# Strassen products for the gates: pairs in one bank, sums of h on VectorE, and transfers for sums sent singly

## The chip, the cores and the metric

The kernel runs on one core of a Trainium2 chip. A core has TensorE (PE in the profile; its weight loads, which overlap the matmuls, are listed as PEld), VectorE (DVE), ScalarE (ACT), GpSimd (POOL) and SyncE (SP), which here only sends transfers. Each engine works through its own list of instructions in order; semaphores hold an instruction back until what it needs is there, and everything behind it on that engine then waits too. Transfers are sent from the queues of SP, ScalarE and GpSimd; those that add to what stands in memory (accumulating transfers) are sent from GpSimd. The metric is device time in microseconds (us); lower is better.

## The reference

One layer of an encoder, for 1024 rows of 1024 float32 numbers:

```python
h = rmsnorm(x, g_mix)
z = h @ w_in                    # columns: 512 pooling, 1024 q, 1024 k, 1024 v
y_pool = pool_mixer(z[:, :512], w_pool_grp, pool_scale)
y_attn = diff_attention(q, k, v, ...)   # 8 heads, two softmax maps each
gates  = sigmoid(h @ w_gate + b_gate)   # 1024x1024 by 1024x2048
merged = gates[:, :1024] * (y_pool @ w_branch_pool) + gates[:, 1024:] * (y_attn @ w_branch_attn)
x = x + merged @ w_out
x = x + square(relu(rmsnorm(x, g_ffn) @ w_up)) @ w_down
```

q and k are normalised by head: each of the 64-element pieces is divided by the root of its mean square plus 1e-6. The change concerns `h @ w_gate` and this head norm.

## The kernel before

**Matmuls.** Each float32 operand is split in two parts of reduced precision, hi (a cast, on ScalarE) and lo (the source less hi, on VectorE unless an engine is given: `split`). A product is three matmuls (`mm3`, lines 140 to 142): hi·hi, hi·lo, lo·hi. All operands have h transposed (`hT[kp, th, hl]`: four pairs of 128-row blocks, two halves of 512 tokens, hi and lo).

**Stages.** The first part, some 710 us, is the attention: a loop over steps `g` = −2 to 73, one step for each of 64 pairs of a head and a tile of 128 tokens. In a step several stages of different tiles are issued, each a fixed number of steps behind the first: `A` computes z (q, k, v of a tile), `B` (`stage_prep`) normalises q and k and splits V, `C` (`stage_qkT`) transposes them, `D` makes scores, `E` transposes the softmax, `F` multiplies with V, `R` normalises. After it come the two branches, the merge with the gates, the output projection and the MLP, which the change leaves alone.

**Fillers.** Between these stages of the attention the loop takes units from a generator, `fillers`, at `F_PACE` units a step from step `F_FROM` on and up to `F_UNITS`; what is left runs behind the loop (the tail). The units are four pooling groups (U, two pairs of units) and the gate products. A scheduler that simulates a timeline then sets each engine's order from all that has been issued.

**The gate products.** `h @ w_gate` is done by Strassen's scheme with 7 products in place of 8 blocks: product 1 to 7 for each of eight column tiles `c`, 12 matmuls of 128x512 each (4 blocks × 3). Products 1, 2 and 3 take blocks of h itself; 5, 6, 7 and 4 take sums of h. The weights of 1, 2 and 4 are blocks of `w_gate`; those of 5, 6, 7 and 3 are sums `gw_sum` 1 to 4, made in memory by a copy (`c`, sent by SP) and an accumulating transfer (`a`, sent by GpSimd; 2 MB each). `h` in `G_SUMS` stores a quarter of h: hi by SP, then lo added by GpSimd. `t_set` (lines 439 and following) loads two such quarters (`rT`), subtracts one from the other on GpSimd and splits the result into the operand `T`, lo on GpSimd too; t6, t4 and t7 build on `t2_dram`, which t5 writes and one accumulating transfer completes.

**What a product does.** `gate_product` loads the weights (`frg`, line 462, on SP), splits them (`fwg`: cast on ScalarE, lo on GpSimd), runs 12 matmuls into one PSUM bank of the fillers, copies the bank to `go` (line 476, ScalarE) and sends it to the quadrants `q` of `gd[c]` that need it: product 1 writes all four (from ScalarE's queue), the others add to what is there (line 483, from GpSimd). `G_TO` says which quadrants. From unit 42 on, a second and third bank are used (`spare_bank`).

**The head norm.** In `stage_prep`, ScalarE squares q and k of a tile (`sq`), VectorE sums each 64 (`ms`), `rsq` multiplies by 1/64 and adds 1e-6 on VectorE (line 282), GpSimd raises to the power −0.5 (line 283), and VectorE multiplies (`qn`, line 801).

```python
O = "B1 C2 H7 D4 R8 E5 F6 W-2 A0"
F_FROM, F_PACE, F_UNITS, F_SPARE = 4, 1.0, 60, 58
```

`O` gives the stages in the order in which a step issues them, with the number of steps by which each lags.

Of the kernel before, what the change touches and what calls it, by code (L numbers as in the profile page):

```python
# [17 lines left out]
P = 128  # L18
# [47 lines left out]
def encoder_kernel(  # L66
# [321 lines left out]
    def gate_sums(what):  # L388

        def wq(i, j):  # L390
            return w_gate[j * 512 : (j + 1) * 512, i * D : (i + 1) * D]

        def copy(i, src):
            with tc.issue_after(marks["SP"]):
                nc.sync.dma_start(gw_sum[i], src)

        def acc(i, src):
            with tc.issue_after(marks["POOL"]):
                nc.gpsimd.dma_start(gw_sum[i], src, accum_op=ALU.add)

        n = int(what[1])
        if what[0] == "h":
            kh, th = divmod(n, 2)
            for hl in range(2):
                for kp in (2 * kh, 2 * kh + 1):
                    dst = h_dram[kh][th][kp % 2 * 256 : kp % 2 * 256 + 256, :].rearrange("(i p) c -> p i c", p=P)
                    with tc.issue_after(marks["POOL" if hl else "SP"]):
                        if hl:
                            nc.gpsimd.dma_start(dst, f(hT[kp, th, 1]), accum_op=ALU.add)
                        else:  # L410
                            nc.sync.dma_start(dst, f(hT[kp, th, 0]))
        elif what[0] == "c":
            copy(what[1], (None, wq(1, 0), gw_sum["1"], wq(1, 0), gw_sum["2"])[n])
        else:
            acc(what[1], (None, wq(1, 1), wq(0, 0), wq(0, 0), wq(0, 1))[n])
# [3 lines left out]
    def t_set(j):  # L419

        for k in range(4):
# [6 lines left out]
            hi, lo = t[:, 0, :], t[:, 1, :]  # L428
            rw = raw([P, S], f"rT{j}_{k}")
            a, b = rw[:, 0:512], rw[:, 512:S]  # L430
            if j == "6":
                nc.sync.dma_start(a, t2_dram[rows, :])
            else:
                sa, sb = {
                    "5": (h_dram[0][0], h_dram[0][1]), "7": (h_dram[1][1], h_dram[0][1]), "4": (t2_dram, h_dram[1][0]),
                }[j]
                nc.sync.dma_start(a, sa[rows, :])
                nc.sync.dma_start(b, sb[rows, :])
                nc.gpsimd.tensor_tensor(a, a, b, op=ALU.subtract)
# [6 lines left out]
    g_unit = [0]  # L446

    def gate_product(j, c):
# [9 lines left out]
        with ExitStack() as later:  # L458
            if n < 3:
                later.enter_context(tc.issue_after(h_hi[n + 2].ins))  # L460
                later.enter_context(tc.issue_after(loads["x3"].ins))
# [3 lines left out]
        ps = (spare_bank if n >= F_SPARE - 16 else fill_bank)(f"g{j}_{c}")  # L465
        for k in range(4):
            if j in "123":
                b = [hT[k // 2 + 2 * (j != "1"), int(j == "3"), hl][:, k % 2, :] for hl in range(2)]
            else:
                b = pair(T[j, k])  # L470
            mm3(ps, w[:, 0, k, :], w[:, 1, k, :], *b, k == 0, k == 3)
        fo = fo_tile(f"go{j}_{c}")
        if j == "6":
            nc.scalar.activation(fo[:, 0:512], ps, AF.Copy, scale=-1.0)
        else:
            nc.scalar.copy(fo[:, 0:512], ps)  # L476
        q0, q1 = G_TO[j]
        dst = gd[c][q0:q1].rearrange("q p t -> p q t")
        from_ = fo[:, 0:512].unsqueeze(1).broadcast_to([P, q1 - q0, 512])
        if j == "1":  # L480
            nc.scalar.dma_start(dst, from_)
        else:
            nc.gpsimd.dma_start(dst, from_, accum_op=ALU.add)  # L483

    def fillers():
        turn, step, groups = {}, 0, 0
        for w in G_PLAN.split():
            if w[0] == "t":
                fw_all[0] = False
                t_set(w[1])  # L490
                continue
            if step in G_SUMS:
                gate_sums(G_SUMS[step])
            step += 1
            if w == "U":
# [3 lines left out]
            else:  # L499
                gate_product(w, turn.setdefault(w, 0))  # L500
                turn[w] += 1
                yield 1
# [4 lines left out]
    with ExitStack() as ph:  # L507
# [282 lines left out]
        def stage_prep(h, t):  # L790
# [19 lines left out]
        def stage_qkT(h, t):  # L810

            th, c0 = t // 4, (t % 4) * P
            if t == 0:
                gghs[h] = sp.tile([P, 1], F32, tag="ggh", name=f"ggh{h}", bufs=2)
# [201 lines left out]
        for g in range(-2, N + 10):  # L1016
# [10 lines left out]
            if g == G_COLS:  # L1027
                columns()
            gens = {}
# [8 lines left out]
            while made < F_UNITS and made < (g - F_FROM) * F_PACE:  # L1038
                made += next(units)
        for _ in units:  # L1040
# [675 lines left out]
```

## Time and profile before

| | |
|---|---|
| time, median of 3 runs | 1572.9 us (1569.59 to 1573.69) |
| the profiled execution | 1573.15 us, span 1571.4 us |
| mean granted TensorE clock | 0.989 |
| busy: TensorE, VectorE, ScalarE, GpSimd | 1520.1, 1075.2, 831.0, 487.7 us |
| transfers | 275.63 MB |

How to read the rows shown below: a row of groups is "line engine operation, out<-in, shape, count | busy us, mean ns | idle time of the engine just ahead of them, and what ended it". A row of waits is "who <- for whom: us in all, count, longest". A row of the chain is "start, length, what", and of the timeline "start, length, what [idle before <- what ended it]". Names are those of the program, with the numbers of buffers left out. A row of transfers ends with KB each and the median us from issue to landing.

### The profile page before, as it was taken

How to read it: one execution, taken by the hardware profiler on the slowest of the kernel's cores; microseconds unless marked ns; L12 is line 12 of the kernel's file. 1: busy time of each engine (PE TensorE's matmuls, PEld its weight loads, DVE VectorE, ACT ScalarE, POOL GpSimd, SP SyncE). 2: the span in 40 equal slices, each digit the busy share in tenths (PEclk: the TensorE clock that was granted, in tenths of full speed). 3: DMA queues.
4: the chain of work that ended last, by engine and by line, in shares of the span. 5: the costliest groups of instructions: out<-in, count | busy, mean ns of one | idle time of the engine just before them, and what ended most of it. 6: DMA issues, size and time to landing. Idle time of an engine off the chain costs nothing.

```text
span 1571.4 us, 21898 instructions
## 1 busy us (share of the span) xinstructions
PE 1520.1 (97%) x7542; PEld 1309.3 (83%) x7542; DVE 1075.2 (68%) x2137; ACT 831.0 (53%) x1717; POOL 487.7 (31%) x515
## 2 busy tenths in 40 slices
PE   9999999999899998988899999999999999999999
PEld 8888988889799987977788887888888878888887
DVE  7687778676677776773474789867675577646662
ACT  6556565564566665664353458556555544333331
POOL 3434334362656455465874630000000000000000
PEclk9999999999999999999999999999999999999999
DMA  7633554386676666479963743555533689637750
GB/s 243 228 75 96 141 184 128 95 194 123 167 157 129 115 128 160 89 180 261 381 220 111 249 161 113 174 169 162 169 137 123 239 300 360 233 129 244 224 199 27
DMA packets 206297, 275.63 MB, mean 175 GB/s; under 512 B 11973, under 2 KB 119210, under 8 KB 206122
## 3 DMA queue, kind: packets, MB, share of 16 engines
q1 hardware_dynamic: 172810, 212.32, 40.8%
q0 software_dynamic: 16336, 34.61, 14.2%
q10 hardware_dynamic: 17040, 27.31, 4.7%
q8 instruction: 59, 0.97, 0.2%
q14 instruction: 52, 0.43, 0.1%
HBM read 186.08 MB, written 105.94 MB: 186 GB/s over the span
## 4 chain that ended last, share of the span: by engine, by line
PE 73%; DMA 9%; DVE 8%; POOL 3%; ACT 3%; issue 3%; SPq 1%; POOLq 0%; ACTq 0%; DVEq 0%
PE z L140 4%; PE z L141 4%; PE z L142 4%; PE Da L141 4%; PE Da L142 4%; PE Da L140 4%; PE Db L142 3%; PE Db L141 3%; PE Db L140 3%; PE X L140 3%; PE X L142 2%; PE X L141 2%; PE g L140 2%; PE g L141 2%; PE g L142 2%
## 5 line engine op out<-in xcount | busy, mean ns | idle before, releaser
L140 PE MATMUL z<-wqkv,hT 128*128 128x384 f32 x512 | 176.6, 345 | 7.1 <-DVE qn L801 6.1
L141 PE MATMUL z<-wqkv,hT 128*128 128x384 f32 x512 | 175.6, 343 | 0.0
L142 PE MATMUL z<-wqkv,hT 128*128 128x384 f32 x512 | 175.3, 343 | 0.0
L876 ACT ACTIVATE s<-s,nm 128x256 f32<-128x256 f32 (+7 forms) x128 | 99.9, 781 | 66.4 <-DVE nm L868 65.7
L283 POOL TENSOR_TENSOR ms<-ms,mhalf 128x4 f32<-128x4 f32 x64 | 68.1, 1064 | 143.5 <-DVE ms L282 140.7
L140 PEld LDWEIGHTS z<-wqkv,hT 128*128 128x128 f32 x512 | 97.8, 191 | 11.8 <-issue 5.7
L141 PEld LDWEIGHTS z<-wqkv,hT 128*128 128x128 f32 x512 | 97.7, 191 | 3.9 <-POOL wqkv L134 0.4
L142 PEld LDWEIGHTS z<-wqkv,hT 128*128 128x128 f32 x512 | 97.5, 191 | 2.8 <-DVE hT L531 0.5
L134 POOL TENSOR_TENSOR fwg<-frg,fwg 128x512 fp32r<-128x512 f32 x56 | 90.1, 1610 | 25.5 <-ACT fwg L133 25.5
L868 DVE CUSTOM_DVE_ANT_0 s<-sc,dist 128x512 f32<-128x512 f32 (+3 forms) x128 | 74.1, 584 | 22.3 <-PE sc L866 17.3
L865 PE MATMUL sc<-K,Q 128*128 128x512 f32 (+2 forms) x192 | 69.4, 363 | 8.5 <-DVE Q L836 6.3
L483 POOL DMA_DIRECT2D gd<-go x48 | 54.6, 1138 | 44.3 <-ACT go L476 26.2
L134 DVE TENSOR_TENSOR AS<-s,AS 128x512 fp32r<-128x512 f32 x64 | 43.4, 687 | 32.7 <-ACT AS L133 32.7
L866 PE MATMUL sc<-K,Q 128*128 128x512 f32 (+2 forms) x192 | 65.3, 347 | 0.0
L134 POOL TENSOR_TENSOR wqkv<-rqkv,wqkv 128x384 fp32r<-128x384 f32 x56 | 61.4, 1194 | 11.5 <-ACT wqkv L133 10.5
L140 PE MATMUL g<-T,fwg 128*128 128x512 f32 x128 | 51.6, 404 | 3.6 <-ACT fwg L133 3.6
L141 PE MATMUL ba<-yT,wba 128*128 128x512 f32 x128 | 50.7, 397 | 4.1 <-DVE yT L134 4.1
L142 PE MATMUL g<-T,fwg 128*128 128x512 f32 x128 | 51.7, 404 | 0.7 <-POOL fwg L134 0.7
L801 DVE TENSOR_TENSOR qn<-z,ms 128x256 f32<-128x256 f32 x64 | 26.9, 420 | 37.2 <-POOL ms L283 22.2
L141 PE MATMUL g<-T,fwg 128*128 128x512 f32 x128 | 51.2, 400 | 0.0
L142 PE MATMUL ba<-yT,wba 128*128 128x512 f32 x128 | 50.5, 395 | 0.0
L921 PE MATMUL ta<-identf,s 128*128 128x128 f32 x288 | 45.4, 276 | 4.9 <-DVE s L885 3.2
(498 smaller groups left out, 4913.3 us busy)
## 6 DMA issues: line engine op xcount, KB each, us to landing
wd<-in_w_down_dram SPq DMA_DIRECT2D x56, 512.0 KB, 5.4
wu<-in_w_up_dram SPq DMA_DIRECT2D x32, 512.0 KB, 4.5
udS<-us SPq DMA_DIRECT2D x64, 256.0 KB, 3.1
ur<-udS SPq DMA_DIRECT2D x32, 512.0 KB, 4.4
rqkv<-in_w_in_dram SPq DMA_DIRECT2D x64, 192.0 KB, 4.6
ur<-ud SPq DMA_DIRECT2D x24, 512.0 KB, 3.5
gd<-go ACTq DMA_DIRECT2D x8, 1024.0 KB, 8.4
gw_sum<-in_w_gate_dram POOLq DMA_DIRECT2D x4, 2048.0 KB, 16.1
```

The source lines that it names most:

```text
L134: (lo_eng or nc.vector).tensor_tensor(lo, src, f(hi), op=ALU.subtract)
L140: nc.tensor.matmul(ps, lhs_hi, rhs_hi, start=first, stop=False, **kw)
L141: nc.tensor.matmul(ps, lhs_hi, rhs_lo, start=False, stop=False, **kw)
L142: return nc.tensor.matmul(ps, lhs_lo, rhs_hi, start=False, stop=last, **kw)
L283: marks["POOL"] = nc.gpsimd.tensor_tensor(dst, dst, mhalf[:, :n], op=ALU.pow).ins
L483: nc.gpsimd.dma_start(dst, from_, accum_op=ALU.add)
L801: nc.vector.tensor_tensor(qn, z[:, 0:256].rearrange("p (a b) -> p a b", a=4), ms.unsqueeze(2).broadcast_to([P, 4, HD]), op=ALU.mult,)
L865: nc.tensor.matmul(dst, Q[:, i, 0, :], rhs, start=True, stop=False)
L866: nc.tensor.matmul(dst, Q[:, i, 1, :], rhs, start=False, stop=True)
L868: nc.vector.tensor_tensor_reduce(out=s[i][:, c : c + w], in0=sc[:, 0:w], in1=dist[:, o0 + c : o0 + c + w], scale=2.0 ** -(h + 1), scalar=B ...
L876: nc.scalar.activation(s[i][:, 0:n], s[i][:, 0:n], AF.Exp, bias=last, scale=-1.0, accum_out=Z[:, i, t : t + 1])
L921: nc.tensor.transpose(ta[:, i * P : (i + 1) * P], a[:, (4 * j + i) * P : (4 * j + i + 1) * P], identf)
```

## The change

1. Two pairs of products share a bank. Products 1 and 2 of a column tile (unit `A`), and products 5 and 3 (unit `B`), run one behind the other: the bank is copied out after the first, and the second then accumulates on top, so that its copy holds their sum. Products 1 and 2 become plain writes from ScalarE's queue (quadrants 1 to 3, and 0); products 5 and 3 add to one quadrant each.
2. `t_set` subtracts and splits on VectorE.
3. The transfers for sums are tied to steps of the main loop (9 to 29), not to units: eight stores of hi (`h`) and eight of lo (`i`) instead of four with two of each, and each weight sum accumulated in two halves of 1 MB.
4. Product 3 comes with product 5, and a unit that does nothing (`.`) stands ahead of each set of sums. Pace 1.03 and 62 units; the spare banks are used in the tail alone.
5. In `stage_prep`, `sq` has a 65th column that holds 1e-6 and stays; the square is scaled by 64 to the power −0.5; the sum over 65 columns is then ready for the power, and the multiply on VectorE is dropped.
6. `ggh` is allocated ahead, with 32 elements of padding: the tiles allocated after it start at a multiple of 64 bytes, where they started 32 bytes off one.

```diff
-F_FROM, F_PACE, F_UNITS, F_SPARE = 4, 1.0, 60, 58
-G_PLAN = "1 1 1 1 U 1 U 1 U 1 U 1 2 2 2 2 2 2 2 2 3 3 t5 3 5 5 5 5 5 5 5 5 t6 3 3 6 6 6 6 6 6 6 6 t4 3 3 4 4 4 4 4 4 4 4 t7 3 7 7 7 7 7 7 7 7"
-G_SUMS = {3: "h0", 5: "c1", 6: "h1", 8: "a1", 10: "h2", 11: "c2", 12: "c3", 13: "h3", 15: "a2", 17: "a3", 18: "c4", 20: "a4"}
-G_TO = {"1": (0, 4), "6": (1, 4), "7": (2, 4), "5": (1, 3), "2": (0, 1), "3": (1, 2), "4": (3, 4)}
+F_FROM, F_PACE, F_UNITS = 4, 1.03, 62
+G_PLAN = "A A A U A U A U A U A A . tB B B B B B B B B . t6 6 6 6 6 6 6 6 6 . t4 4 4 4 4 4 4 4 4 . t7 7 7 7 7 7 7 7 7"
+G_SUMS = {
+    9: "h0", 10: "i0 c1", 11: "h1", 12: "i1 a10", 13: "a11", 14: "h2", 15: "i2 c2", 16: "h3", 17: "i3 c3", 18: "a20",
+    19: "a21", 20: "h4", 21: "i4 a30", 22: "a31", 23: "h5", 24: "i5 c4", 25: "h6", 26: "i6 a40", 27: "a41", 28: "h7", 29: "i7",
+}
+G_TO = {"1": (1, 4), "2": (0, 1), "6": (1, 4), "7": (2, 4), "5": (2, 3), "3": (1, 2), "4": (3, 4)}
...
+            r = slice(int(what[2]) * 256, int(what[2]) * 256 + 256)
             with tc.issue_after(marks["POOL"]):
...
+                nc.gpsimd.dma_start(gw_sum[what[1]][r, :], src[r, :], accum_op=ALU.add, max_dma_last_dim=1024)
...
-                nc.gpsimd.tensor_tensor(a, a, b, op=ALU.subtract)
+                nc.vector.tensor_tensor(a, a, b, op=ALU.subtract)
             if j == "5":
                 nc.sync.dma_start(t2_dram[rows, :], a)
-            split(hi, lo, a, nc.gpsimd)
+            split(t[:, 0, :], t[:, 1, :], a)
...
+    def gate_unit(js, c):
+
+        ws = [gate_weights(j, c) for j in js]
+        ps = (spare_bank if in_tail[0] else fill_bank)(f"g{js}_{c}")
+        for n, (j, w) in enumerate(zip(js, ws)):
+            for k in range(4):
...
+                mm3(ps, w[:, 0, k, :], w[:, 1, k, :], *b, k == 0 and n == 0, k == 3, n > 0)
+            fo = fo_tile(f"go{j}_{c}")
...
+            if j in "12":
+                nc.scalar.dma_start(dst, from_)
+            else:
+                nc.gpsimd.dma_start(dst, from_, accum_op=ALU.add)
...
+            elif w == ".":
+                yield 1
...
+        sq = sp.tile([P, 4, HD + 1], F32, name="sq")
+        nc.gpsimd.memset(sq[:, :, HD : HD + 1], EPS)
...
+            gghs[h] = sp.tile([P, 1], F32, tag="ggh", name=f"ggh{h}", bufs=2)
+            if h == 0:
+                pad(sp, 32)
...
-            sq = s1([P, 256], F32, f"sq{h}_{t}", "sq")
             ms = sp.tile([P, 4], F32, tag="ms", name=f"ms{h}_{t}", bufs=3)
-            nc.scalar.activation(sq, z[:, 0:256], AF.Square)
-            nc.vector.tensor_reduce(ms, sq.rearrange("p (a b) -> p a b", a=4), axis=AX.X, op=ALU.add)
-            rsq(ms, ms, 4, 1.0 / HD)
+            nc.scalar.activation(
+                sq[:, :, 0:HD], z[:, 0:256].rearrange("p (a b) -> p a b", a=4), AF.Square, scale=HD ** -0.5
+            )
+            nc.vector.tensor_reduce(ms, sq, axis=AX.X, op=ALU.add)
+            marks["POOL"] = nc.gpsimd.tensor_tensor(ms, ms, mhalf[:, 0:4], op=ALU.pow).ins
...
+            for what in G_SUMS.get(g, "").split():
+                gate_sums(what)
```

How the order moves, at two places. In the rows, the first number behind a name is its product, head or sum, and the last a buffer. First SyncE before, from the last weights of product 2 to the first of product 5 (`gw_sum4` is the copy for the sum that product 3 uses):

```order
L462 DMA frg2_7_4545<-in_w_gate_dram 128x4x128
L529 DMA rqkv5_0_4723<-in_w_in_dram 128x3x128 x2
L529 DMA rqkv5_1_4732<-in_w_in_dram 128x3x128 x2
L395 DMA gw_sum4_139<-gw_sum2_137 32x16384
L462 DMA frg3_0_4676<-gw_sum4_139 128x4x128
L462 DMA frg3_1_4793<-gw_sum4_139 128x4x128
L462 DMA frg3_2_4954<-gw_sum4_139 128x4x128
L462 DMA frg5_0_5052<-gw_sum1_136 128x4x128
L529 DMA rqkv5_2_4741<-in_w_in_dram 128x3x128 x2
```

SyncE now, at the copy for the same sum:

```order
L532 DMA rqkv3_1_2758<-in_w_in_dram 128x3x128 x2
L322 DMA frpool2_1_2824<-in_w_in_dram 128x4x128
L409 DMA gw_sum4_139<-gw_sum2_137 32x16384
L355 DMA rgrp2_2829<-in_w_pool_grp_dram 128x128
L460 DMA frg1_5_3303<-in_w_gate_dram 128x4x128
```

And at the first weights of products 5 and 3:

```order
L460 DMA frg2_7_4268<-in_w_gate_dram 128x4x128
L532 DMA rqkv4_2_3746<-in_w_in_dram 128x3x128 x2
L532 DMA rqkv4_3_3755<-in_w_in_dram 128x3x128 x2
L460 DMA frg5_0_4634<-gw_sum1_136 128x4x128
L460 DMA frg3_0_4639<-gw_sum4_139 128x4x128
L435 DMA rT5_0_4602<-h_dram00_140 128x512
L436 DMA rT5_0_4602<-h_dram01_141 128x512
```

The copy for the fourth sum has moved from right ahead of the first load that uses it to the time of the third pooling group, with the weights of two more tiles of products 1 and 2 and those of a whole head between.

Second, GpSimd before, at the sums of h for product 4 (`rT4`):

```order
L483 DMA gd5_133<-go6_5_6878 128x3x512
L134 TENSOR_TENSOR fwg6_7_7096<-frg6_7_7094,fwg6_7_7096 128x512
L134 TENSOR_TENSOR wqkv7_6_6692<-rqkv7_3_6689,wqkv7_6_6692 128x384
L134 TENSOR_TENSOR wqkv7_7_6695<-rqkv7_3_6689,wqkv7_7_6695 128x384
L439 TENSOR_TENSOR rT4_0_7192<-rT4_0_7192 128x512
L483 DMA gd6_134<-go6_6_6976 128x3x512
L134 TENSOR_TENSOR fwg3_5_7221<-frg3_5_7219,fwg3_5_7221 128x512
L439 TENSOR_TENSOR rT4_1_7199<-rT4_1_7199 128x512
L908 MEMSET AT6_2_4_7016 128x128 x2
L283 TENSOR_TENSOR ms7_0_6980<-ms7_0_6980,mhalf_102 128x4
```

GpSimd now, at the same place:

```order
L487 DMA gd2_130<-go6_2_6759 128x3x512
L137 TENSOR_TENSOR fwg6_4_6974<-frg6_4_6972,fwg6_4_6974 128x512
L137 TENSOR_TENSOR wqkv7_5_6569<-rqkv7_2_6563,wqkv7_5_6569 128x384
L137 TENSOR_TENSOR wqkv7_6_6575<-rqkv7_3_6572,wqkv7_6_6575 128x384
L137 TENSOR_TENSOR wqkv7_7_6578<-rqkv7_3_6572,wqkv7_7_6578 128x384
L487 DMA gd3_131<-go6_3_6856 128x3x512
L137 TENSOR_TENSOR fwg6_5_7069<-frg6_5_7067,fwg6_5_7069 128x512
L916 MEMSET AT6_2_4_6894 128x128 x2
L807 TENSOR_TENSOR ms7_0_6859<-ms7_0_6859,mhalf_102 128x4
```

And VectorE now:

```order
L437 TENSOR_TENSOR rT4_0_7486<-rT4_0_7486 128x512
L137 TENSOR_TENSOR AT6_1_0l_6683<-ta6_3_0_6781,AT6_1_0h_6682 128x4x128
L891 RECIPROCAL cf6_4_6813<-Z6_5868 128x1
L892 SCALAR_TENSOR_TENSOR cf6_4_6813<-cf6_4_6813,Z6_5868,nlam_386 128x1
L437 TENSOR_TENSOR rT4_1_7493<-rT4_1_7493 128x512
L893 SCALAR_TENSOR_TENSOR s6_4_0_6774<-s6_4_1_6775,cf6_4_6813,s6_4_0_6774 128x640
L876 ISA s6_5_0_6885,nm6_5_6887<-sc6_5_0_0_6888,dist_383 128x512
L876 ISA nm6_5_6887 128x1
L806 TENSOR_REDUCE ms7_0_6859<-sq_387 128x4
L137 TENSOR_TENSOR V7_0_6790<-z7_0_6795,V7_0_6790 128x128
```

The two sums have left GpSimd's list, where the power of the head norm (`ms7_0`) stood behind them, for VectorE's, where the softmax of head 6 (`s6_4`, `s6_5`), the reduction for `ms7_0` and the split of `V7_0` stand behind them.

More of the change, by code (lines that the diff above doesn't have):

```diff
@@ L391, in wq @@
             return w_gate[j * 512 : (j + 1) * 512, i * D : (i + 1) * D]
-        def copy(i, src):
+        n = int(what[1])
+        if what[0] in "hi":
+            kp, th = n // 2, n % 2
+            dst = h_dram[kp // 2][th][kp % 2 * 256 : kp % 2 * 256 + 256, :].rearrange("(i p) c -> p i c", p=P)
+            if what[0] == "i":
+                with tc.issue_after(marks["POOL"]):
+                    nc.gpsimd.dma_start(dst, f(hT[kp, th, 1]), accum_op=ALU.add)
+            else:
+                with tc.issue_after(marks["SP"]):
+                    nc.sync.dma_start(dst, f(hT[kp, th, 0]))
+        elif what[0] == "c":
+            src = (None, wq(1, 0), gw_sum["1"], wq(1, 0), gw_sum["2"])[n]
             with tc.issue_after(marks["SP"]):
-                nc.sync.dma_start(gw_sum[i], src)
-        def acc(i, src):
+                nc.sync.dma_start(gw_sum[what[1]], src)
+        else:
+            src = (None, wq(1, 1), wq(0, 0), wq(0, 0), wq(0, 1))[n]
+            r = slice(int(what[2]) * 256, int(what[2]) * 256 + 256)
             with tc.issue_after(marks["POOL"]):
[L399 to L415, printed above, removed]
+                nc.gpsimd.dma_start(gw_sum[what[1]][r, :], src[r, :], accum_op=ALU.add, max_dma_last_dim=1024)
     T = {}
@@ L489, in fillers @@
                 fw_all[0] = False
[L490 to L495, printed above, removed]
+                t_set(w[1].replace("B", "5"))
+            elif w == ".":
+                yield 1
+            elif w == "U":
                 for _ in pool_group(groups):
@@ L1039, in encoder_kernel @@
                 made += next(units)
+        in_tail[0] = True
         for _ in units:
```

47 lines of the change are left out of this document (20 added, 27 removed).

## The prediction

> **What bounds the kernel now.** I read the page's totals, then the busy time by stage, then the chain of waits at the two longest stops of TensorE, and last the groups and transfers that the change touches.
>
> ```profile
> span 1571.4 us, 21898 instructions
> PE 1520.1 (97%) x7542; PEld 1309.3 (83%) x7542; DVE 1075.2 (68%) x2137; ACT 831.0 (53%) x1717; POOL 487.7 (31%) x515
> 0.00:720.00 720.00, 682.71 (x3839) 619.25 (x3840) 531.54 (x1436) 426.80 (x1061) 347.76 (x416) 0.98 0.61 148
> 720.00:790.00 70.00, 63.09 (x266) 50.49 (x266) 28.64 (x30) 29.53 (x55) 53.22 (x39) 0.95 1.00 322
> 790.00:1571.00 781.00, 774.32 (x3441) 639.52 (x3439) 514.99 (x671) 374.71 (x602) 86.71 (x62) 1.00 0.55 187
> ```
>
> The last three rows give, by stretch, the busy time of TensorE, its weight loads, VectorE, ScalarE and GpSimd, then the granted clock, the transfers' share and GB/s. The profiled run took 1573.15 us, 1.75 around its span, and lies 0.25 above the median of 1572.9. TensorE sets the time. From 790 us on it idles 6.7 us at full clock, and the change touches nothing there. In the first 720 us, where all edits lie, it idles 37.3 us (720.00 − 682.71) at a clock of 0.98. A change that leaves the matmuls as they are can win only there: 37.3 us, and at most (1 − 0.98) × 720 = 14 us of lost clock. So I looked for single stops. The longest two are 5 us each.
>
> Chain, first stop (start, length, what):
>
> ```profile
> 381.30 16.37 DMA gw_sum<-in_w_gate_dram
> 397.72 2.87 DMA frg<-gw_sum
> 400.62 0.63 ACT fwg L133
> 401.29 0.80 PE g L140
> 401.29 0.80 PE L140 MATMUL g<-hT,fwg 128*128 128x512 f32 x1 [5.02 <-ACT fwg L133]
> SPq L462 <- DMA gw_sum<-in_w_gate_dram: 52.0, 1, 52.0
> 380.00:400.00 20.00, 16.27 (x107) 15.68 (x105) 7.32 (x24) 5.58 (x16) 4.38 (x6) 0.98 0.71 133
> 400.00:420.00 20.00, 18.58 (x84) 16.19 (x85) 13.49 (x36) 14.36 (x38) 17.55 (x20) 0.85 0.56 148
> ```
>
> The fourth weight sum ends its accumulation at 397.7, SP's queue has stood 52.0 us before the first load of product 3's weights, ScalarE's cast waits for that load with the rest of its queue behind it, and TensorE idles 5.02 us. The clock afterwards is 0.85 for 20 us. Stop and clock cost 5.0 + 0.02 × 20 + 0.15 × 20 = 8.4 us. [...]
>
> Chain, second stop:
>
> ```profile
> 588.90 12.05 DMA rT<-h_dram
> 601.12 1.26 POOL rT L439
> 602.66 1.02 POOL ms L283
> 603.70 0.43 DVE qn L801
> 604.27 0.66 PE z L140
> 604.27 0.66 PE L140 MATMUL z<-wqkv,hT 128*128 128x384 f32 x1 [5.35 <-DVE qn L801]
> 600.00:620.00 20.00, 15.73 (x83) 14.68 (x84) 12.87 (x38) 9.80 (x21) 14.70 (x14) 0.91 0.58 136
> 583.94 1.30 POOL L483 DMA_DIRECT2D gd<-go  x1
> 589.25 1.76 POOL L483 DMA_DIRECT2D gd<-go  x1
> rT<-h_dram SPq DMA_DIRECT2D x20, 256.0 KB, 3.9
> gd<-go POOLq DMA_DIRECT2D x8, 768.0 KB, 8.5
> ```
>
> Here the operand for a sum of h takes 12.05 us where such a load takes 3.9 in the median: two results of product 6, three quadrants each, were sent out at 583.94 and 589.25. GpSimd stands before the sum, the norm's power (L283) waits behind it, and TensorE idles 5.35 us. With 0.09 × 20 of clock this stop costs 7.1 us.
>
> **The change part by part.**
>
> ```profile
> POOL rT L439 <- DMA rT<-h_dram: 16.4, 6, 8.8
> L439 POOL TENSOR_TENSOR rT<-rT 128x512 f32<-128x512 f32 x12 | 17.2, 1434 | 16.5 <-DMA rT<-h_dram 16.4
> L134 POOL TENSOR_TENSOR T<-rT,T 128x512 fp32r<-128x512 f32 x16 | 21.9, 1398 | 4.2 <-ACT T L133 4.2
> L134 DVE TENSOR_TENSOR mix<-sum,mix 128x512 fp32r<-128x512 f32 x8 | 5.5, 684 | 0.1
> L134 DVE TENSOR_TENSOR ypT<-rypT,ypT 128x512 fp32r<-128x512 f32 x8 | 9.4, 1204 | 5.9 <-ACT ypT L133 5.9
> PE 73%; DMA 9%; DVE 8%; POOL 3%; ACT 3%; issue 3%; SPq 1%; POOLq 0%; ACTq 0%; DVEq 0%
> L282 DVE TENSOR_SCALAR ms<-ms 128x4 f32<-128x4 f32 x64 | 15.0, 234 | 0.2
> L283 POOL TENSOR_TENSOR ms<-ms,mhalf 128x4 f32<-128x4 f32 x64 | 68.1, 1064 | 143.5 <-DVE ms L282 140.7
> L884 DVE SCALAR_TENSOR_TENSOR cf<-cf,Z,nlam 128x1 f32<-128x1 f32 x64 | 36.8, 574 | 1.6
> L483 POOL DMA_DIRECT2D gd<-go x48 | 54.6, 1138 | 44.3 <-ACT go L476 26.2
> L399 POOL DMA_DIRECT2D gw_sum<-in_w_gate_dram x4 | 4.5, 1120 | 0.0
> gw_sum<-in_w_gate_dram POOLq DMA_DIRECT2D x4, 2048.0 KB, 16.1
> L476 ACT COPY go<-g 128x512 f32<-128x512 f32 x48 | 28.2, 588 | 17.3 <-PE g L142 14.4 <-DMA gd<-go 1.5 <-ACT fwg L133 0.9
> L945 ACT ACTIVATE oq<-po 128x256 f32<-128x256 f32 x31 | 11.8, 381 | 2.0 <-PE po L142 1.9
> L946 ACT COPY oS<-po 128x256 f32<-128x256 f32 x31 | 11.4, 367 | 0.0
> ```
>
> Weight sums earlier. They are tied to steps of the main loop. The last half of the fourth sum is now sent at step 27. Ahead of product 3's first load the plan holds 33 units, which at 1.03 a step are used up by step 36; 720 us over some 72 steps make 10 us a step, so some 90 us lie between, against 16.1 for a whole sum. SP no longer stands before it, and the 8.4 us of the first stop go. What is late next there would be the sum of h for product 5; its operands are stored by step 17, 19 steps ahead. The price: four accumulations become eight of half the size, four more issues × 1.12 = 4.5 us of GpSimd, which is 52% idle there (347.8 of 720). The transfers move into the first 300 us, where loads of wqkv run beside them. If they make no load late the cost is 0; if they do, it is another stop like the first, +8.4. I take 0, the nearer row being the single load of 3.9 us, which is sent a step of ten us ahead.
>
> Sums of h on VectorE. GpSimd loses 12 × 1.434 + 16 × 1.398 = 39.6 us. VectorE has the like at 0.684 us (the mix split, alone) and at 1.204 (the ypT split, beside GpSimd): 28 × 0.684 = 19.2 us, or 28 × 1.204 = 33.7. I take the lower one, as GpSimd has less beside it. The mean norm multiply at L282 goes from VectorE, 64 × 0.234 = 15.0 us, its work being done in the square's scale and a 65th column. Net VectorE gets 4.2 to 18.7 us on 531.5 of 720, that is 74% to at most 76.4% busy. VectorE's 8% of the chain are 0.08 × 1571 = 126 us, 12% of its 1075 us of work. At that share the dropped multiply is worth −1.8 us and the moved work +2.3 to +4.0. I take 0, since much of the moved work stands where TensorE has products of other kinds left to do; bounds −1.8 and +4.0.
>
> The waits for the operands are another matter. The sums carry 16.4 us of waiting over 6 occurrences, 8.8 of it in one. They now stand in VectorE's queue, with the split of A, the score epilogue, the norm's reduction and the V split behind the second sum for product 4. A wait there reaches TensorE sooner than from GpSimd. In the new order the two loads again run beside three-quadrant results of product 6, one sent ahead of the first sum, one between. The pause ahead of the sum delays the next products by one step, not the transfers. So the second stop is the one I do not know. It goes (−7.1), stays (0), or takes the other 16.4 − 8.8 = 7.6 us along, with a clock window of half speed lost (0.09 to 0.17 × 20 = 1.8 to 3.4): up to +11.0. I take 0, the middle value: same load, same neighbours, a wait moved from one queue to another.
>
> Products that share a bank. The matmuls are the same; 56 copies out of the bank stay, at 0.588 us each. The second product of a pair waits for the copy of the first, as the next product already does with one bank (17.3 us of waits of ScalarE there stand for TensorE's own work). GpSimd issues 8 fewer accumulations × 1.138 = 9.1 us, and the accumulated quadrants fall from 10 to 8 for each of eight columns, 20 to 16 MB. Issue and transfers lie beside TensorE: 0. A second write of one quadrant moves to ScalarE's queue, 8 issues, hidden by its 41% idle (426.8 of 720): 0.
>
> Pauses and pace. Twelve units were left for the tail, thirteen products are now; one product more of 12 matmuls moves from the attention to its tail, where it takes the same TensorE time: 0. Aligned tiles: the two copies at L945 and L946 read the same bank, one into an aligned and one into an unaligned tile, and take 381 and 367 ns: 0.
>
> Sum: 1573.15 − 8.4 + 0 + 0 + 0 = 1564.75; less the 0.25 by which the profiled run lies above the median, 1564.5 us.
>
> **The rivals.**
>
> First, more gain. The second stop goes too, since the result traffic is 20% less and GpSimd's power is no longer behind the sum: 1564.5 − 7.1 = 1557.4. A third stop lies at 328 to 332 us in a row of 0.83, where the old second and third sums were accumulated:
>
> ```profile
> 320.00:340.00 20.00, 17.39 (x77) 14.48 (x76) 15.02 (x32) 11.71 (x30) 12.67 (x16) 0.83 0.75 150
> ```
>
> TensorE idles 2.61 there and loses 3.4 of clock; without it, 1551.4. Against it: the row's transfers at 0.75 have other owners too.
>
> Second, no difference. The sums and singly spread stores of h crowd the first 300 us, one load comes 8 us late, and the 8.4 us return elsewhere: 1573. For it: a load did take 12.05 against 3.9. Against: halves of 1 MB hold the queues for a shorter time than 16.1 us.
>
> Third, slower. VectorE stands before the sums of products 5, 4 and 7, in order, and everything of the attention stands behind it: +11.0 at the second stop, and another stop of 5 like the known ones at the first sum for product 5: 1564.5 + 16 = 1580.5. It decides from a load about 4 us late: the 8.8 us of waiting on GpSimd stopped TensorE for 5.35, so some 3.4 were bridged. Against it: the other five waits, 7.6 us together, gave no stop of that size.
>
> Fourth, the moved operations are held by GpSimd's: 28 × (1.204 − 0.684) = 14.6 us of VectorE, all on the path: 1564.5 + 14.6 = 1579. The row L884 speaks for it, with 574 ns for one element a partition where L282 takes 234 for four; against it, what GpSimd loses (39.6 us) was just such work. [...]
>
> **How the numbers follow.** Chances: the forecast 0.38 (1560 to 1568), more gain 0.21, no difference 0.22, slower by waits 0.14, held by GpSimd 0.05. Faster than the median by over 0.3% (4.7 us, about what a measurement tells from no change) are the first two: 0.58 after rounding off their edge; same 0.23, slower 0.19. The likeliest case's own range is 1560 to 1568; the range to 8 in 10 leaves out the far end of both sides: 1552, where all three stops are gone, to 1579.
>
> **What would show it.** In the profile after: no wait of SP for a sum of some tens of us, and no stop of TensorE of 5 us before product 3, confirm the first term. VectorE's waits for loads of rT show the second: if they sum to about 16 us with one of over 8, it stays; if GpSimd's row L134 of T is gone and VectorE's is near 0.7 us, the fourth is wrong. Busy TensorE in the first 720 us should stay near 683 less lost clock. I am wrong if the loads for sums of h wait longer than 12 us, or if a new stop of over 3 us stands between 120 and 300 us.

## The result, and the profile after

The changed kernel takes 1551.9 us (median of 4, 1549.99 to 1553.23) against 1572.9: a ratio of 0.987, 95% interval 0.9852 to 0.9887. That is faster, as forecast, but 20.9 us faster where 8.4 were forecast, and just outside the range (1552 to 1579). It comes out where the first rival stood (1551.4), but only in part by that rival's stops: the one before product 3 and the one near 330 us are gone, the second stop stayed.

The page and the stretches of after, with the same columns as before, and behind them the same stretches of before in the finer cut that is used from here on (0 to 340, 340 to 450 and so on, us from the start):

```profile
span 1551.5 us, 21873 instructions
PE 1516.4 (98%) x7542; PEld 1303.3 (84%) x7542; DVE 1069.1 (69%) x2101; ACT 829.2 (53%) x1717; POOL 460.5 (30%) x484
0.00:340.00 340.00, 333.05 (x1906) 302.47 (x1906) 258.55 (x701) 210.22 (x532) 159.73 (x211) 1.00 0.68 174
340.00:450.00 110.00, 108.93 (x630) 100.27 (x629) 80.20 (x224) 64.25 (x162) 44.69 (x52) 1.00 0.43 91
450.00:640.00 190.00, 183.96 (x1059) 168.03 (x1059) 137.85 (x386) 115.14 (x294) 84.09 (x95) 0.99 0.54 116
640.00:740.00 100.00, 89.44 (x411) 71.82 (x410) 59.58 (x111) 53.06 (x108) 53.74 (x48) 0.93 0.91 228
740.00:960.00 220.00, 215.22 (x964) 176.94 (x964) 159.83 (x217) 115.88 (x229) 118.28 (x82) 0.98 0.58 196
```

```profile
0.00:340.00 340.00, 322.58 (x1810) 291.75 (x1811) 258.01 (x702) 199.28 (x506) 139.76 (x200) 0.98 0.53 149
340.00:450.00 110.00, 104.62 (x598) 96.58 (x597) 76.08 (x219) 62.42 (x156) 55.34 (x62) 0.97 0.73 164
450.00:640.00 190.00, 182.36 (x1047) 167.77 (x1046) 139.31 (x378) 114.16 (x287) 107.46 (x111) 0.99 0.65 131
640.00:740.00 100.00, 90.33 (x463) 76.55 (x462) 62.48 (x149) 59.04 (x131) 59.99 (x58) 0.97 0.79 186
740.00:960.00 220.00, 215.42 (x967) 177.62 (x967) 146.33 (x193) 106.08 (x204) 124.24 (x88) 0.98 0.65 217
```

TensorE runs the same 7542 matmuls. Length less busy time is its idle time; over the whole span it falls from 51.3 to 35.1 us, and busy time by 3.7 us, beside a mean granted clock of 0.992 where it was 0.989. The idle time by stretch:

| us from start | 0–340 | 340–450 | 450–640 | 640–740 | 740–960 |
|---|---|---|---|---|---|
| before: idle, clock | 17.4, 0.98 | 5.4, 0.97 | 7.6, 0.99 | 9.7, 0.97 | 4.6, 0.98 |
| after: idle, clock | 7.0, 1.00 | 1.1, 1.00 | 6.0, 0.99 | 10.6, 0.93 | 4.8, 0.98 |

Most of the gain lies ahead of 340 us, in stops that the prediction didn't look at one by one: five of 1.1 to 3.2 us, and many under 1 us. TensorE's longest waits there in the kernel before, and what stands behind the second and the third of them:

```profile
PE sc L865 <- DVE Q L836: 4.1, 2, 3.2
PE g L140 <- ACT go L476: 3.5, 2, 2.6
PE ta L921 <- DVE AT_0l L134: 1.7, 1, 1.7
50.73 0.62 ACT L133 CAST fwpool<-frpool 128x512 fp32r<-128x512 f32 x1 [3.95 <-DMA frpool<-in_w_in_dram]
81.91 3.46 DVE L884 SCALAR_TENSOR_TENSOR cf<-cf,Z,nlam 128x1 f32<-128x1 f32 x1
```

ScalarE stands 3.95 us at a cast for its load, with the copy `go` that TensorE wants behind it (2.6 us). VectorE spends 3.46 us on one `cf`, of which the median is 0.22 us, with the split of `AT_0l` behind it (1.7 us). The stop before product 3 is gone. From 640 to 960 us, after is no better.

### The profile page after: what moved, and what is told of

Read it like the earlier page. It is cut to its first block, busy times and chain, and to the rows that moved or that the text cites. A ratio compares the mean times of both kernels' runs of the same rounds, so it can differ in the third digit from the quotient of the medians.

```text
span 1551.5 us, 21873 instructions
## 1 busy us (share of the span) xinstructions
PE 1516.4 (98%) x7542; PEld 1303.3 (84%) x7542; DVE 1069.1 (69%) x2101; ACT 829.2 (53%) x1717; POOL 460.5 (30%) x484
## 5 line engine op out<-in xcount | busy, mean ns | idle before, releaser
L143 PE MATMUL z<-wqkv,hT 128*128 128x384 f32 x512 | 173.7, 340 | 1.1 <-ACT wqkv L136 0.8
L145 PE MATMUL z<-wqkv,hT 128*128 128x384 f32 x512 | 174.7, 341 | 0.0
L144 PE MATMUL z<-wqkv,hT 128*128 128x384 f32 x512 | 173.6, 339 | 1.0 <-POOL wqkv L137 1.0
L143 PEld LDWEIGHTS z<-wqkv,hT 128*128 128x128 f32 x512 | 96.5, 189 | 5.2 <-ACT wqkv L136 1.3
L144 PEld LDWEIGHTS z<-wqkv,hT 128*128 128x128 f32 x512 | 96.5, 189 | 5.1 <-POOL wqkv L137 2.0
L145 PEld LDWEIGHTS z<-wqkv,hT 128*128 128x128 f32 x512 | 96.5, 189 | 3.1 <-DVE hT L534 0.5
L876 DVE CUSTOM_DVE_ANT_0 s<-sc,dist 128x512 f32<-128x512 f32 (+3 forms) x128 | 74.2, 584 | 14.1 <-PE sc L874 11.8
L487 POOL DMA_DIRECT2D gd<-go x40 | 43.0, 1076 | 71.3 <-ACT go L480 44.3
L137 POOL TENSOR_TENSOR wqkv<-rqkv,wqkv 128x384 fp32r<-128x384 f32 x56 | 60.5, 1178 | 10.5 <-ACT wqkv L136 6.9
L137 POOL TENSOR_TENSOR wo<-ro,wo 128x512 fp32r<-128x512 f32 x28 | 41.0, 1480 | 28.7 <-ACT wo L136 27.3
```

Source lines behind the costliest of these rows:

```text
L137: (lo_eng or nc.vector).tensor_tensor(lo, src, f(hi), op=ALU.subtract)
L143: nc.tensor.matmul(ps, lhs_hi, rhs_hi, start=first, stop=False, **kw)
L144: nc.tensor.matmul(ps, lhs_hi, rhs_lo, start=False, stop=False, **kw)
L145: return nc.tensor.matmul(ps, lhs_lo, rhs_hi, start=False, stop=last, **kw)
L876: nc.vector.tensor_tensor_reduce(out=s[i][:, c : c + w], in0=sc[:, 0:w], in1=dist[:, o0 + c : o0 + c + w], scale=2.0 ** -(h + 1), scalar=B ...
```

## The experiments

All ratios are to runs of the kernel before on the same chip, with 95% intervals.

**One part of the change undone, or one done alone.** Late sums in the changed kernel:

```diff
-    9: "h0", 10: "i0 c1", 11: "h1", 12: "i1 a10", 13: "a11", ... 26: "i6 a40", 27: "a41", 28: "h7", 29: "i7",
+    8: "h0 h2 i0 i2", 13: "c1", 14: "h1 h3 i1 i3", 19: "a10 a11", 24: "h4 h6 i4 i6", 28: "c2", 29: "c3",
+    30: "h5 h7 i5 i7", 31: "a20 a21", 32: "a30 a31", 33: "c4", 34: "a40 a41",
```

> The changed kernel with the stores of h and the weight sums sent at about the steps at which the kernel before sent them (the last accumulation two steps ahead of product 3). Theory A (the early transfers carry most of the gain: besides the stop before product 3 they take away small stops in the first 340 us): about 1566 us, with stops of TensorE of 2 us and more again between 200 and 340 us or before product 3. Theory B (the shorter head norm and the lighter GpSimd carry what the stop before product 3 does not): the stop of 8 us alone comes back, about 1560. Theory C (the order that the scheduler finds moves several us with any edit): anywhere from 1552 to 1570, with stops at places that have nothing to do with the sums.

Measured: 1574.9 us, 1.0008 (0.9988 to 1.0027). The whole gain is gone, more than theory A had. Its longest stop, in TensorE's, ScalarE's and SyncE's lists, and its waits:

```profile
SPq L409 <- DMA gw_sum<-in_w_gate_dram: 34.0, 1, 34.0
311.27 0.47 SPq L409 DMA_DIRECT2D gw_sum<-gw_sum  x1
311.84 7.88 SPq L532 DMA_DIRECT2D rqkv<-in_w_in_dram  x4
326.37 0.51 ACT L136 CAST wqkv<-rqkv 128x384 fp32r<-128x384 f32 x1 [11.98 <-DMA rqkv<-in_w_in_dram]
326.93 0.69 PE L143 MATMUL z<-wqkv,hT 128*128 128x384 f32 x1 [8.15 <-ACT wqkv L136]
```

The copy for a sum (L409) takes the previous sum, so it waits on SyncE until that has been accumulated, 34 us here. Loads of wqkv stand behind it. ScalarE reaches the cast of these 12 us before the load lands, and TensorE stops for 8.15. Cut at 310 us, ahead of its first long stop, the first 450 us read:

```profile
0.00:310.00 310.00, 305.50 (x1756) 280.13 (x1757) 234.17 (x644) 192.77 (x486) 142.62 (x191) 1.00 0.56 152
310.00:450.00 140.00, 119.20 (x648) 109.01 (x647) 85.84 (x238) 70.66 (x177) 55.84 (x64) 0.91 0.66 150
```

Ahead of 310 us it idles 4.5 us, less than the changed kernel (6.4) and the kernel before (14.8). From 310 to 450 us it idles 20.8, where these two idle 1.7 and 8.0. So the small stops of the first 310 us do not come back with the late sums; the loss lies behind them.

The early transfers alone, put into the kernel before (the new table and `gate_sums`, nothing else):

> The kernel before with only the early, single transfers for sums (the table of steps 9 to 29 and the halves). Theory A: about 1559 us (14 less than before), the stops at 230 and 330 us gone too. Theory B: about 1564.5, the 8.4 of the stop before product 3. Theory C: 1558 to 1572, with new stops elsewhere.

Measured: 1.0016 (0.9996 to 1.0036), no gain. The stop before product 3 is gone, but 340 to 450 us idles 5.3 us as before (5.4), in smaller stops, and the first 340 us idle 19.1 us where they idled 17.4, with a stop of 2.7 us near 125 us that is new. So the early sums are not enough; A and B both fail on it.

The short head norm alone, put into the kernel before:

> The kernel before with only the short head norm (scaled square, 65th column, no multiply on VectorE). If the shorter norm stands by itself (taking it away from the changed kernel cost 5 us): about 1568 us, the loss falling in the first 340 us. If it gains only where the transfers are early too: 1573, within 3.

Measured: 1.0000 (0.9978 to 1.0021); idle in the first 340 us 14.0, in 340 to 450 8.6. And both together in the kernel before:

> The kernel before with the early single transfers and the short head norm together (each alone gave 1.00). Theory D (the two work only together, since each loss has both a late transfer and a late norm behind it): about 1555 us. Theory E (the plan is needed: pairs and pooling groups in the new order, product 3 behind the sums for product 5): still 1568 to 1573.

Measured: 1.0030 (1.0012 to 1.0048). Theory D falls. The profile names one stop, again from SyncE to TensorE:

```profile
SPq L409 <- DMA gw_sum<-in_w_gate_dram: 59.9, 2, 40.7
119.69 0.48 SPq L409 DMA_DIRECT2D gw_sum<-gw_sum  x1
120.27 0.54 SPq L461 DMA_DIRECT2D frg<-in_w_gate_dram  x1
129.75 0.62 ACT L136 CAST fwg<-frg 128x512 fp32r<-128x512 f32 x1 [13.96 <-DMA frg<-in_w_gate_dram]
131.33 0.80 PE L143 MATMUL yp<-mix,wgrp 128*128 128x512 f32 x1 [10.77 <-ACT mix L136]
```

The load of product 1's next weights stands behind the copy for the second sum. ScalarE waits 14 us at its cast, although what TensorE wants next (`mix`) is another cast, behind it in the same list.

**The place of the copies.** The same kernel with the copies for sums 2 and 4 one load of weights later in SyncE's list (steps 19 and 29 for 15 and 24, with the accumulations behind them moved along):

> The kernel before with early transfers and the short norm, as in the run that gave 1.003, but with the copies for the second and fourth weight sum one load of weights later in SyncE's list, so that no load that is needed at once stands behind a copy that waits for an accumulation. Theory F (a copy that waits on SyncE holds the loads behind it, and that is what the old plan lost): the stop of 10.8 us at 120 is gone, about 1558 us. Theory E (the plan matters in some other way): 1568 or more.

Measured: 1570.8 us, 0.9988 (0.9965 to 1.0010), against 1.0030. The intervals lie apart, just: some 7 us by the ratios, which is no more than order alone can do (below). So it is the stop that counts here, and not the time. SyncE now sends the load first:

```profile
SPq L409 <- DMA gw_sum<-in_w_gate_dram: 11.3, 1, 11.3
111.54 0.37 SPq L461 DMA_DIRECT2D frg<-in_w_gate_dram  x1
123.21 0.48 SPq L409 DMA_DIRECT2D gw_sum<-gw_sum  x1
121.76 0.62 ACT L136 CAST fwg<-frg 128x512 fp32r<-128x512 f32 x1 [3.54 <-DMA frg<-in_w_gate_dram]
```

The stop of 10.8 is gone, as theory F has it. But 17.1 us of idle time in the first 340 us remain, with a stop of 4.2 us near 238 us, so F is a part and not the whole.

**The order of the first units.** The kernel with early transfers and the short norm (1.0030), and this line:

```diff
-G_PLAN = "1 1 1 1 U 1 U 1 U 1 U 1 2 2 2 2 2 2 2 2 3 3 t5 ...
+G_PLAN = "1 2 1 2 1 2 U 1 2 U 1 2 U 1 2 U 1 2 1 2 3 3 t5 ...
```

> The kernel before with early transfers, the short norm, and the order of units 1 2 1 2 1 2 U 1 2 U 1 2 U 1 2 U 1 2 1 2 for its first part (products keep their own banks, the rest of the plan and the pace stay). If the order of the first units is what the early transfers needed: idle and lost clock in the first 340 us fall from 32 us (the same without the new order) to 10 or less, and the time to about 1555. If it is something else in the plan: 20 or more and 1568.

Measured: 1552.7 us, 0.9875 (0.9860 to 0.9889): the changed kernel's gain, with banks of their own, sums of h on GpSimd, no alignment, no pauses, the old pace and product 3 in its old place. Its first stretches:

```profile
0.00:340.00 340.00, 332.92 (x1910) 306.98 (x1911) 254.50 (x711) 209.24 (x531) 161.91 (x216) 0.99 0.67 169
340.00:450.00 110.00, 107.07 (x610) 96.57 (x609) 72.90 (x204) 63.80 (x159) 55.02 (x58) 1.00 0.53 124
```

Idle 7.1 in the first 340 us, where the same kernel in the old order had 21.6. The old order has a pooling group after every one product, the new one after two, and products 2 no longer come in a block of eight. Which of the two it is was not tried.

**What each part does, by place.** TensorE's idle time, in us, ahead of 310 us and from there to 450. The cut at 310 us was chosen from the traces, ahead of the first long stop that the late sums leave:

| kernel | first units | sums | 0–310 | 310–450 | both |
|---|---|---|---|---|---|
| before | old order | late | 14.8 | 8.0 | 22.8 |
| before, pace 1.03 (below) | old order | late | 11.3 | 13.1 | 24.4 |
| before, short norm | old order | late | 8.9 | 13.8 | 22.6 |
| before, early sums | old order | early | 17.7 | 6.8 | 24.4 |
| before, early sums and short norm | old order | early | 20.2 | 4.0 | 24.2 |
| the same, copies later | old order | early | 15.5 | 4.0 | 19.5 |
| changed, late sums | new order | late | 4.5 | 20.8 | 25.3 |
| before, early sums, short norm, new order | new order | early | 7.1 | 2.9 | 10.0 |
| changed | new order | early | 6.4 | 1.7 | 8.0 |
| changed, own banks (below) | new order | early | 8.5 | 2.0 | 10.5 |
| changed, multiply back, pace 1.03 (below) | new order | early | 8.5 | 1.5 | 10.0 |

The new order lowers the idle time ahead of 310 us, with late sums too. The early sums lower it behind 310 us, in the old order too. Either without the other leaves some 19.5 us or more in all; all twelve kernels that have both, in four different orders, idle 6.4 to 12.6 us. The short norm alone comes near the new order ahead of 310 us (8.9) and loses it again behind; as the last row shows, the gain doesn't need it.

**Parts that turned out free.** Alignment, shared banks, and pauses, each undone in the changed kernel (the padding left out; products 1, 2, 5, 3 in banks of their own with the old `G_TO`; the four "." taken out and 58 units):

> The changed kernel without the padding, so that the tiles behind it lie 32 bytes off a multiple of 64 again. If alignment is free, as the two copies of before had it (367 and 381 ns): the same mean durations, about 1552 us give or take the 4 us by which a new order moves. If it carries part of the gain: longer operations on qn, Q, oS and rT and over 1556.

> The changed kernel in which products 1, 2, 5 and 3 each have a bank and quadrants of their own again (1 writes four quadrants, 2, 5 and 3 accumulate as in the kernel before), in the changed order. If shared banks are free, as predicted: about 1552 us. If the 8 accumulations and 4 MB less matter for GpSimd's queue or the transfers: 1558 to 1562, with longer waits for loads of rT and rqkv.

> The changed kernel without the four units that do nothing (62 becomes 58 units). If the pauses are idle as predicted: about 1552 us. If they give the sums of h the time to load: waits of VectorE for rT well above 11 us in all, and 1556 to 1560.

Measured: 0.9871 (0.9846 to 0.9896), 0.9902 (0.9880 to 0.9924) and 0.9847 (0.9802 to 0.9891), next to 0.987 (0.9852 to 0.9887). Without the padding the durations are the same to a nanosecond or two. First the changed kernel, then the one without:

```profile
L810 DVE TENSOR_TENSOR qn<-z,ms 128x256 f32<-128x256 f32 x64 | 26.9, 420 | 14.7 <-POOL ms L807 7.1 <-PE tk L830 7.1
L954 ACT COPY oS<-po 128x256 f32<-128x256 f32 x32 | 11.8, 368 | 0.0
```

```profile
L808 DVE TENSOR_TENSOR qn<-z,ms 128x256 f32<-128x256 f32 x64 | 26.8, 419 | 14.0 <-PE tk L828 7.2 <-POOL ms L805 6.4
L952 ACT COPY oS<-po 128x256 f32<-128x256 f32 x32 | 11.8, 368 | 0.0
```

Own banks are 3.1 us slower by the medians, which the intervals, and the next part, do not tell from nothing.

**What order alone does.** The changed kernel with a pace of 1.02 for 1.03:

> The changed kernel with a pace of 1.02 for 1.03, which leaves the work and its transfers as they are and moves units by one step here and there from step 37 on. What it differs by from 1551.9 is what order alone does: within 4 us if single edits can be read to that size; 5 to 10 if they cannot.

Measured: 1543.2 us, 0.9802 (0.9767 to 0.9837), 8.7 us less by the medians from moving a few units by a step. So no single edit to the changed kernel can be read to better than that from its time alone. The kernel before, with its pace alone changed:

> The kernel before with a pace of 1.02 for 1.0 and nothing else. If order alone moves the kernel before as it moved the changed one (8.7 us): a ratio off 1 by 0.004 or more to either side. If before is no odd draw: 0.997 to 1.003.

> The kernel before with the pace of the changed one, 1.03, and nothing else. If the kernel before is an odd draw: about 1560, like pace 1.02. If 1.02 was a lucky one: 1570 or more.

Measured: 1558.2 us, 0.9912 (0.9881 to 0.9944) at 1.02 and 1557.9 us, 0.9905 (0.9888 to 0.9921) at 1.03. In the kernel before the pace alone is worth 15 us (both values take one unit more at the first step of the fillers and run ahead from there). The profile of pace 1.03, for the same stretches and its waits for sums of h:

```profile
0.00:340.00 340.00, 323.24 (x1822) 293.40 (x1823) 250.63 (x703) 199.21 (x507) 142.50 (x200) 0.98 0.55 156
340.00:450.00 110.00, 102.32 (x580) 94.03 (x579) 74.61 (x221) 61.93 (x154) 52.09 (x59) 0.95 0.60 136
450.00:640.00 190.00, 187.99 (x1087) 172.56 (x1086) 135.49 (x380) 117.42 (x293) 115.84 (x119) 1.00 0.71 141
740.00:960.00 220.00, 220.00 (x1004) 182.71 (x1003) 166.99 (x210) 116.76 (x230) 127.14 (x86) 1.00 0.60 210
POOL rT L439 <- DMA rT<-h_dram: 6.3, 5, 1.6
PE g L140 <- ACT fwg L133: 10.3, 2, 5.1
```

It gains behind 450 us (2.0 idle for 7.6, and none for 4.6 from 740 to 960), where the sums for product 4 meet no late load. It keeps the idle time of the first 340 us (16.8) and the stop before product 3 (5.1). So the pace gains at another place than the change, which idles 21.4 us from 450 to 960 us where the kernel before idles 21.9 and this one 10.8. Whether the pace itself does it or the order that came of it is open. It speaks for the pace that the four other kernels above in the old plan at 1.0 idle 18.5 to 21.6 us there, and against it that the changed kernel has the same pace.

**VectorE's two parts.** Sums of h on GpSimd, or the norm's multiply on VectorE again, in the changed kernel at both paces, and both at once at 1.03:

```diff
-                nc.vector.tensor_tensor(a, a, b, op=ALU.subtract)
+                nc.gpsimd.tensor_tensor(a, a, b, op=ALU.subtract)
-            split(t[:, 0, :], t[:, 1, :], a)
+            split(t[:, 0, :], t[:, 1, :], a, nc.gpsimd)
```

```diff
-            marks["POOL"] = nc.gpsimd.tensor_tensor(ms, ms, mhalf[:, 0:4], op=ALU.pow).ins
+            rsq(ms, ms, 4, 1.0 / HD)
```

> The changed kernel with the sums of h and their lo split back on GpSimd. Theory A: about 1553 us, since the stop at product 4's sums costs the same on either engine (5.2 us on VectorE now, 7.1 on GpSimd before). Theory B: about 1558, the norm's power standing behind the sums again. Theory C: 1548 to 1558.

> The changed kernel with the pace of 1.02 (1543.2 us) and the sums of h on GpSimd. If the sums cost 8 us on VectorE: 1535. If what they gave at the pace of 1.03 was order: 1543 within 4.

> The changed kernel with the multiply of the head norm back on VectorE (64 x 0.234 us). Theory A: about 1554 us. Theory B: about 1560, with more small stops of TensorE behind qn, Q and AT. Theory C: 1548 to 1560.

> The changed kernel with the pace of 1.02 (1543.2 us) and the norm's multiply back on VectorE. If the multiply costs 5 us or more: 1548 to 1553, with the loss again in the first 340 us. If it was order: 1543 within 4.

> The changed kernel with both VectorE parts undone: sums of h on GpSimd and the norm's multiply back on VectorE; the new plan, the pairs, the early transfers and the alignment stay. Theory E: about 1549 us (1543.7 of the kernel with sums on GpSimd, plus the 5 of the norm). Theory D: 1560 or more.

| | pace 1.03 | pace 1.02 |
|---|---|---|
| the changed kernel | 1551.9, 0.987 (0.9852–0.9887) | 1543.2, 0.9802 (0.9767–0.9837) |
| sums of h on GpSimd | 1543.7, 0.9809 (0.9772–0.9845) | 1545.1, 0.9828 (0.9798–0.9859) |
| multiply on VectorE | 1556.9, 0.9899 (0.9864–0.9934) | 1554.5, 0.9890 (0.9855–0.9925) |
| both | 1557.8, 0.9892 (0.9854–0.9930) | not run |

The engine of the sums: 8.2 us better on GpSimd at one pace, 1.9 worse at the other. So these runs cannot tell the engine's part from that of the order. The multiply: worse each time, by 5.0, 11.3 and (beside sums on GpSimd) 14.1 us by the medians. In the first 340 us these three idle 10.0, 10.6 and 10.1, and the kernels without it 7.0, 6.2 and 6.6, so 3.0 to 4.4 us of the loss lie there. But these are not six cases. By the names of its operations, TensorE's list up to some 320 us is one and the same in the three with the multiply, and another one in the three without: two orders, measured three times each. The first has two stops of some 2.1 us that the second hasn't. At the pace of 1.03 the first of them, and what stands behind the second, are:

```profile
38.95 0.21 PE L749 MATMUL cols_ps<-identf,rows 32*128 32x32 f32 x1 [2.13 <-issue]
151.96 5.96 DVE L890 SCALAR_TENSOR_TENSOR cf<-cf,Z,nlam 128x1 f32<-128x1 f32 x1
```

The first waited for nothing that the profile shows. At the second TensorE stops 2.05 us at 159 for `Q`, whose operation stands in VectorE's list behind a `cf` of 5.96 us (5.5 and 6.1 in the other two; the changed kernel has one of 4.5 there, and no stop over 0.4). Neither waited for the multiply. What the multiply costs by itself is not shown.

**A version that beats both.** Sums on GpSimd without pauses:

> The changed kernel with the sums of h on GpSimd and without pauses. If the two single gains (8.3 and 5.6 us) add up: 1538. If the second was a matter of order alone: 1543 within 4.

Measured: 1544.7 us, 0.9806 (0.9775 to 0.9837). The single gains do not add up. It, the pace of 1.02 and the sums on GpSimd all beat both kernels, at 1543 to 1545 us; the runs do not tell one of them from another.

## Why the prediction was wrong, point by point

- **Where TensorE can win.** Right that all of it lies in the idle time and the clock of the attention. The step that failed is the next one: "So I looked for single stops. The longest two are 5 us each." The 17.4 us of the first 340 us, in stops of up to 3.2 us, got no term but for the one near 330 us, which stood in a rival, and the change took 10.5 of them away, with the lost clock beside them (0.98 to 1.00 of 340 us). Nor did the new order of products 1 and 2 and the pooling groups get a term, which the runs show to take most of these stops away.
- **The weight sums earlier (−8.4).** Right in mechanism and size for its stretch: 340 to 450 us goes from 5.4 idle at 0.97 to 1.1 at 1.00, about 4.3 + 3.3 = 7.6 us. Every kernel run with late sums has the stop, or one of its kind; none of those with early sums stops longer than 2.5 us there. But the term was counted as if it stood alone. Put into the kernel before, the early sums give nothing. With the short norm beside them the reason shows: SyncE waits earlier, and a load that is needed stands behind (10.8 us). "If they make no load late the cost is 0" was the point, and whether they do depends on the order of the units. In the kernel with the early sums alone SyncE waits for sums 23.5 us, much as before (22.3), and what costs the time there stays open.
- **The head norm (0 together with the moved sums, bounds −1.8 to +4.0).** Not settled. Alone in the kernel before the short norm gives nothing; taken out of the changed kernel it costs 5 to 14 us by the medians, more than the bounds, but the only difference that shows at one place is 3.0 to 4.4 us in one pair of orders, and its two stops do not wait for the multiply.
- **The second stop (0).** Right, with luck: 0 was the middle of three cases, from −7.1 to +11.0, and not worked out. The half speed in the last of them is what the kernel before shows behind this stop: a granted clock of 0.50 from 604 to 606 us and of 1.00 from 608. VectorE waits for the loads where GpSimd did, and TensorE stops 1.36 and 2.16 us, at a clock of 0.91 as before: 5.3 us where it was 7.1.

```profile
DVE rT L437 <- DMA rT<-h_dram: 11.0, 6, 3.2
568.85 0.69 DVE L437 TENSOR_TENSOR rT<-rT 128x512 f32<-128x512 f32 x1 [5.29 <-DMA rT<-t_dram]
570.20 0.39 PE L144 MATMUL po<-AT_0l,V 128*128 128x256 f32 x1 [1.36 <-DVE AT_0l L137]
572.47 0.69 DVE L437 TENSOR_TENSOR rT<-rT 128x512 f32<-128x512 f32 x1 [2.00 <-DMA rT<-h_dram]
574.11 0.63 PE L929 MATMUL ta<-identf,s 128*128 128x128 f32 x4 [2.16 <-DVE s L893]
560.00:580.00 20.00, 16.47 (x89) 14.73 (x88) 9.50 (x25) 9.48 (x25) 8.21 (x10) 0.91 0.77 165
```

- **Sums of h on VectorE (19.2 us of busy time, 0 on the path).** Right. The 28 operations take 8.3 + 10.9 = 19.2 us, each near 0.69 us, so the fourth rival (held by GpSimd at 1.2) is wrong. Its price of 1.204 us was a mean of unlike operations: of the eight ypT splits of before, seven took 0.68 to 0.77 us and one 4.75, with two of GpSimd's splits beside it. First the changed kernel, then before, with the shortest, the median and the longest in ns:

```profile
L437 DVE TENSOR_TENSOR rT<-rT 128x512 f32<-128x512 f32 x12 | 8.3, 693 | 16.2 <-DMA rT<-h_dram 11.0 <-DMA rT<-t_dram 5.3
L137 DVE TENSOR_TENSOR T<-rT,T 128x512 fp32r<-128x512 f32 x16 | 10.9, 686 | 2.3 <-ACT T L136 2.3
L134 DVE TENSOR_TENSOR ypT<-rypT,ypT x8: 677/686/4752, 701.3 to 718.9; 128x512 fp32r<-128x512 f32 x8
```

Five of the 28 overlapped with a TENSOR_TENSOR of GpSimd, for 0.2 to 0.7 us, and took 0.68 to 0.74 us; the other 23 took 0.68 to 0.69. So these overlaps cost nothing that shows.

- **Shared banks, alignment (0).** Right, within what the runs can tell.
- **Pace and pauses (0).** Wrong for the pace, which counted no change of order: 15 us in the kernel before, and 8.7 in the changed one between 1.03 and 1.02.
- **The rivals.** More gain came true in size, but its place was the whole of the first 340 us, of which the stop at 328 us is one part, and not the second stop. The second rival (sums and stores that "crowd the first 300 us", and the time comes back elsewhere) came true for the early sums in the old order; where a cause shows, it is SyncE's wait and not the transfers' load.

How it adds up: the order of the first units and the early sums make the gain, and only together; what the short norm adds is open. From 450 us on the changed kernel gains little and has a new stop behind 740 (3.24 us at the first `oX`, behind VectorE's merge):

```profile
880.04 0.76 PE L143 MATMUL oX<-wo,A 128*128 128x512 f32 x1 [3.24 <-DVE mp L1056]
```

Against the kernel before at the pace of 1.03 (0.9905), the whole change at the same pace (0.987) is worth some 6 us by the medians; at 1.02 it is 0.9802 against 0.9912, 15 to 17 us. Why the late stretches turn out well or badly for a pace is open beyond the stops named.

## What to carry to other kernels

A transfer that waits for another transfer on a queue that also feeds casts held everything behind it here (34.0 us on SyncE with the late sums, and TensorE stopped for 8.15): read what stands next in that list, not only whether the transfer is early enough. Add up small stops by stretch before choosing the two long ones. And where a scheduler sets the order, run a neutral edit (a pace of 1.02) first: here it moved as much as most edits, so only effects that show in the same stretch in several kernels can be believed, and only if these kernels differ in their order there.

## What the runs showed of the hardware that was not expected

Three sizes were not expected. VectorE's `cf` takes 0.22 us in the median, but single ones took 3.46 us in the kernel before, 4.47 in the changed one and 5.96 in the one with the multiply back, each beside three to seven TENSOR_TENSORs of GpSimd in a row. Of the 32 in before that had none beside them, the longest took 0.25. Two of the small stops shown above stand behind such a one. ScalarE, with 426.8 of 720 us busy in the kernel before, passed most of a late load on, its cast standing in one list with TensorE's next operand: 14.0 us of its waiting gave 10.8 of TensorE's (kernel before with early sums and the short norm). And the 2 MB copy from one sum to the next, which is sent early, kept SyncE standing for 65.2 us in the changed kernel without a stop of TensorE:

```profile
SPq L409 <- DMA gw_sum<-in_w_gate_dram: 65.2, 2, 36.5
121.11 0.47 SPq L409 DMA_DIRECT2D gw_sum<-gw_sum  x1
128.90 0.37 SPq L460 DMA_DIRECT2D frg<-in_w_gate_dram  x1
```

The first load of weights behind the first of these copies is sent 8 us after it, and TensorE has no stop over 0.4 us from 80 to 230 us.
